# Differential attention scores on Trainium2: from 32-row fp32 products to full-height products of placed parts

## The chip, the cores and the metric

The kernel runs on one core of one Trainium2 chip. The metric is the device time of one execution in microseconds; kernels are compared by the medians of runs.

## What the kernel computes

Two transformer blocks, each two layers deep, follow one another. The first block works on 256 tokens of `x` and 256 tokens of `ctx`, 1024 features wide, in fp32. Each of its layers has a mixer with three kinds of attention heads ("a" grouped-query, "b" neighbourhood, "c" differential), and then a feed-forward network with a short convolution. The second block (FoX attention, gated linear attention and two feed-forward networks a layer) is not touched by the change.

The change concerns the four heads of kind "c". Each has two maps of 32 features, and its output is the difference of two softmaxes:

```python
def diff_attend(q, kvs, lam, scale):
    s = jnp.concatenate([jnp.einsum('bhmqd,bhmkd->bhmqk', q, k, ...) for k, _ in kvs], axis=-1) * scale
    p = jax.nn.softmax(s, axis=-1)
    w = p[:, :, 0] - lam * p[:, :, 1]
    ...
```

The 256 queries of `x` attend to the 512 keys of `x` and `ctx`; in layer 0 the 256 queries of `ctx` also attend to the 256 keys of `ctx`. In layer 1 `ctx` asks nothing.

## The kernel before

**Layout and precision.** Activations lie feature by feature: a tile has 128 features on the partitions and up to 512 tokens in its columns. A product that needs more than the reduced fp32r type gives is made of parts: `split` writes a high part (ScalarE, a copy into fp32r) and a low part (VectorE, the value less the high part). A projection of 1024 features takes 24 fp32r products (`mm1`, L269 to L271): high by high, high by low, low by high, for each of 8 blocks of 128 features. `weight` loads a block of weights on SP's queue and splits it (L261 on ScalarE, L262 on VectorE); there are four buffers of each.

**The heads of kind "c".** A tile of queries, `qc`, and one of keys, `kc`, hold two heads of two maps: 4 groups of 32 partitions. `qk` normalises and rotates them: a square (L447) and a copy (L448) on ScalarE, a product with a block matrix (L450), the root (L315 to L324), a multiplication (L452) and the rotation (L455 to L458, two of these on GpSimd). `values` copies the values to SBUF (L465), transposes them (L468) and evacuates them (`evac`, L357 on ScalarE and L359 on VectorE in turn).

**The attend loop.** `attend` runs for two heads, and in each for two blocks of 128 queries, and in layer 0 for the queries of `ctx` as well. For each of these it makes the scores of both maps (L528), the softmaxes and their difference (`weigh`: L478 to L498 on VectorE and ScalarE), calls `fill`, transposes the weights (L551, L569) and copies them out (L554, L572); at the end the weights meet the values (L579, L586). In kind "c" a score is one plain fp32 product of a 32-row slice. In the kinds "b" and "a" it is two fp32r products over 128 rows (L531, L532), of high and low parts that `stack` puts above one another with ScalarE and VectorE alone.

**What sets the order.** The first six projections run as one `gemm`. The other twelve are a generator, `project`; `fill` takes the next of them, 24 products long, wherever an attend would leave TensorE without work, and steps of the modulation (`ada_step`, L372) when there are none left. Within that the order of each engine's instructions is laid down before the run by a planner. It goes by the program's order and by the costs that it assumes, takes an instruction that is ready where an earlier one isn't, and hands out buffers. Tiles come from pools: 18 tiles of "q" (the projected tiles and stacked parts), 9 of "t" (short-lived), and in PSUM 5 banks of "mm" (projections, scores) and 3 of "at".

**The start.** `first` loads the inputs and constants, runs sixteen steps of the modulation, and then loads the first three weights of layer 0.

Of the kernel before, what the change touches and what calls it, by code (L numbers as in the profile page):

```python
# [10 lines left out]
F32R = mybir.dt.float32r  # L11
U8 = mybir.dt.uint8
AF = mybir.ActivationFunctionType
ALU = mybir.AluOpType
AX = mybir.AxisListType
P = 128
# [169 lines left out]
class Kern:  # L186
# [314 lines left out]
    def stack(self, o, n, keys):  # L501
# [13 lines left out]
                nc.scalar.activation(kl[hh][x], kl[hh][r].bitcast(F32), AF.Copy)  # L515
        return (st, kl) if keys else st

    def attend(self, l, kind, q, k, v, with_ctx, bias=None, lam=None):

        nc = self.nc  # L520
        ident = self.con("ident")
        pts = []

        def scores(sp, hh, i, qs, ks, last):

            if kind == "c":
                p0 = 64 * hh + 32 * i
                nc.tensor.matmul(sp, q[p0:p0 + 32, qs], k[p0:p0 + 32, ks], start=True, stop=last)  # L528
                return
            st, kl = k  # L530
            nc.tensor.matmul(sp, q[hh][:, qs], st[hh][:, ks], start=True, stop=False)  # L531
            nc.tensor.matmul(sp, q[hh][:, qs], kl[hh][:, ks], start=False, stop=last)  # L532

        for hh in range(2):
            maps = range(2 if kind == "c" else 1)
            px = [self.n().rearrange("p (k t) -> p k t", k=2) for _ in range(2)]
            for qi in range(2):
                sps = []
                for i in maps:
                    sp = self.mmp()  # L540
                    scores(sp, hh, i, slice(qi * P, (qi + 1) * P), slice(0, 512), bias is None)
                    if bias is not None:
                        for rr in range(2):
                            nc.tensor.matmul(sp[:, rr * P:(rr + 1) * P], self.con("rev"), bias(qi, rr, hh), start=False,
                                             stop=rr == 1)
                    sps.append(sp)
                pm = self.weigh(sps, 1, 512, lam)
                self.fill(l)
                tp = self.atp()
                for kc in range(4):  # L550
                    nc.tensor.transpose(tp[:, kc * P:(kc + 1) * P], pm[:, kc * P:(kc + 1) * P], ident)  # L551
                tv = tp.rearrange("p (k t) -> p k t", k=4)
                for i in range(2):
                    nc.vector.tensor_copy(px[i][:, :, qi * P:(qi + 1) * P], tv[:, 2 * i:2 * i + 2])  # L554
            pcx = None
            if with_ctx:
                sps = []
                for i in maps:
                    sp = self.mmp()
                    for qi in range(2):  # L560
                        scores(sp[:, qi * 256:(qi + 1) * 256], hh, i, slice(256 + qi * P, 256 + (qi + 1) * P),
                               slice(256, 512), True)
                    sps.append(sp)
                pm = self.weigh(sps, 2, 256, lam)
                self.fill(l)
                tp = self.atp()
                for kc in range(2):
                    for qi in range(2):
                        nc.tensor.transpose(tp[:, kc * 256 + qi * P:kc * 256 + (qi + 1) * P],  # L569
                                            pm[:, qi * 256 + kc * P:qi * 256 + (kc + 1) * P], ident)  # L570
                pcx = self.n()
                nc.vector.tensor_copy(pcx, tp)  # L572
            pts.append((px, pcx))
        po = self.atp()
        for kc in range(4):
            for hh, (px, pcx) in enumerate(pts):
                r0 = 64 * hh
                vv = v[:, kc * P + r0:kc * P + r0 + 64]
                nc.tensor.matmul(po[r0:r0 + 64, :256], vv, px[kc // 2][:, kc % 2], start=kc == 0,  # L579
                                 stop=kc == 3 and not with_ctx)  # L580
        if with_ctx:
            for kc in range(2):
                for hh, (px, pcx) in enumerate(pts):
                    r0 = 64 * hh
                    vv = v[:, (2 + kc) * P + r0:(2 + kc) * P + r0 + 64]
                    nc.tensor.matmul(po[r0:r0 + 64, 256:512], vv, pcx[:, kc * 256:(kc + 1) * 256], start=False, stop=kc == 1)  # L586
        return po[:, :512 if with_ctx else 256]
# [18 lines left out]
    def first_layer(self, l):  # L606
        nc, A = self.nc, self.A
# [73 lines left out]
        O = [None] * 8  # L681
        order = []
        for j in range(2):
            po = self.attend(l, "c", get("qc", j), get("kc", j), get("vc", j), wc, lam=lam)
            O[6 + j] = self.parts(self.subln(po, nq, gains["g_subln"]))
            order.append(6 + j)
        for j in range(2):
# [103 lines left out]
    def first(self, ctx):  # L791
        nc, A = self.nc, self.A
        p1 = self.p1 = self.pool(ctx, "first", 1)
        self.CON1 = p1.tile([P, NCON1], F32, name="CON1")
        self.LAM = p1.tile([P, 256], F32, name="LAM")
        self.C = p1.tile([P, KC, TC], F32, name="C")
        self.MOD = [p1.tile([P, 48, 2], F32, name=f"MOD{l}") for l in range(2)]
        self.CS = p1.tile([P, KC, 32], F32, name="CS")
        cs = self.t()[:, :KC * 32]
        nc.sync.dma_start(cs, A["ccT"].rearrange("p c i -> p (c i)"))  # L800
        nc.sync.dma_start(self.H, A["hT"])
        nc.sync.dma_start(self.C, A["cT"])
        nc.sync.dma_start(self.CON, A["con"])
        nc.sync.dma_start(self.VEC, A["vec"])
        nc.scalar.activation(self.CS.rearrange("p c i -> p (c i)"), cs, AF.Silu)
        self.table_exp()
        st = [self.stat_new(256, nc.vector), self.stat_new(256)]
        for c in range(KC):
            self.stat_add(st[0], self.H[:, c, TM:TH])
            self.stat_add(st[1], self.C[:, c, :])  # L810
        self.G1, self.G2 = {}, {}
        self.known, self.mods = -1, self.ada()
        for i in range(16):
            next(self.mods)
            if i == 7:
                with self.tc.issue_after(self.last_ada):
                    zs = [self.stat_end(s) for s in st]
                self.xn = [self.n() for _ in range(KC)]
                for c in range(KC):
                    nc.vector.tensor_tensor(self.xn[c][:, :256], self.H[:, c, TM:TH], zs[0], ALU.mult)  # L820
                    nc.vector.tensor_tensor(self.xn[c][:, 256:], self.C[:, c, :], zs[1], ALU.mult)
        self.head = [self.weight(A["w1_in"][0, j]) for j in range(3)]
        nc.sync.dma_start(self.CON1, A["con1"])
        nc.sync.dma_start(self.LAM, bass.AP(A["lamv"].tensor, 0, [[0, P], [1, 256]]))

        self.first_layer(0)
        self.first_layer(1)
# [493 lines left out]
```

## Time and profile before

| | |
|---|---|
| runs of the kernel | 2429.46 us median of 3 (2428.62 to 2435.38) |
| profiled execution | 2433.39 us; span from the first to the last instruction 2431.6 us |
| TensorE busy | 2320.8 us, 16128 matmul records |
| VectorE, ScalarE busy | 1523.2 us, 1270.2 us |
| mean granted clock of TensorE | 0.98 |
| scores of kind "c" | 82.4 to 187 us (layer 0), 762.6 to 819 us (layer 1) |

PE is TensorE, PEld its weight load, DVE VectorE, ACT ScalarE, POOL GpSimd, SP the queue that starts most transfers. L528 is line 528 of the kernel. Records of matmuls overlap, since the next starts while the last drains; what one costs in a row of them is the distance between starts.

### The profile page before, as it was taken

To read this page: it belongs to the slowest core of one execution; us is meant where nothing else is said; L and a number is where in the kernel's file an instruction comes from. 1 tells how busy PE (TensorE), PEld (TensorE's weight loads), DVE (VectorE), ACT (ScalarE), POOL (GpSimd) and SP (SyncE) were. 2 spreads that over 40 slices of the span, in tenths; PEclk is the share of its full clock that TensorE was granted. 3 is DMA by queue.
4 is the path that set the end of the run, shared out by engine and by line. 5 is a ranking of instruction groups with operands and counts; after the bars stand their busy time and mean duration, and the time that the engine had idled before them with its cause. 6 is when DMAs were issued, how large, how long until landed. Compare 5 with 4: busy or idle time off the path is not lost. (4 is left out here: it accounts for less than half of the span.)

```text
span 2431.6 us, 40872 instructions
## 1 busy us (share of the span) xinstructions
PE 2320.8 (95%) x16128; PEld 2043.5 (84%) x16128; DVE 1523.2 (63%) x2605; ACT 1270.2 (52%) x2196; POOL 401.7 (17%) x417
## 2 busy tenths in 40 slices
PE   5999999999999989999999999899999999998998
PEld 3665677778877758999999988899989999888997
DVE  4667665444547776776664876676466557666664
ACT  3658644333346775664444545554454444466553
POOL 0300021000022001211111320321121122113111
PEclk8999999999999999999999999999999999999999
DMA  7313335433233246556555533445545545334653
GB/s 269 103 37 131 113 130 173 139 121 96 93 117 120 71 156 211 194 177 191 183 168 180 167 106 105 148 157 174 174 148 178 169 147 195 104 114 149 196 180 118
DMA packets 100993, 358.57 MB, mean 147 GB/s; under 512 B 11488, under 2 KB 12864, under 8 KB 100544
## 3 DMA queue, kind: packets, MB, share of 16 engines
q1 hardware_dynamic: 98640, 349.82, 44.4%
q0 software_dynamic: 1792, 5.53, 0.9%
q8 instruction: 127, 2.08, 0.4%
q10 hardware_dynamic: 368, 0.59, 0.1%
q14 instruction: 66, 0.54, 0.1%
HBM read 354.83 MB, written 1.07 MB: 146 GB/s over the span
## 5 line engine op out<-in xcount | busy, mean ns | idle before, releaser
L269 PE MATMUL mm_t<-n_t,hi_t 128*128 128x272 f32 (+2 forms) x3600 | 1112.4, 310 | 25.4 <-ACT n_t L839 18.7
L270 PE MATMUL mm_t<-n_t,hi_t 128*128 128x272 f32 (+2 forms) x3600 | 1109.5, 308 | 6.0 <-DVE n_t L840 5.0
L271 PE MATMUL mm_t<-n_t,lo_t 128*128 128x272 f32 (+2 forms) x3600 | 1106.0, 308 | 1.1 <-DVE lo_t L262 1.1
L262 DVE TENSOR_TENSOR lo_t<-raw_t,hi_t 128x1024 fp32r<-128x1024 f32 (+1 forms) x574 | 713.2, 1246 | 391.2 <-ACT hi_t L261 387.1
L261 ACT ACTIVATE hi_t<-raw_t 128x1024 fp32r<-128x1024 f32 (+1 forms) x574 | 595.5, 1039 | 680.6 <-PE mm_t L270 509.4
L269 PEld LDWEIGHTS mm_t<-n_t,hi_t 128*128 128x128 f32 x3600 | 686.0, 191 | 77.7 <-ACT n_t L839 20.9
L270 PEld LDWEIGHTS mm_t<-n_t,hi_t 128*128 128x128 f32 x3600 | 688.5, 191 | 38.1 <-DVE n_t L840 8.4
L271 PEld LDWEIGHTS mm_t<-n_t,lo_t 128*128 128x128 f32 x3600 | 687.9, 191 | 33.0 <-issue 5.8
L269 PE MATMUL mm_t<-q_t,hi_t 128*128 128x272 f32 (+2 forms) x896 | 274.6, 307 | 0.7 <-ACT q_t L306 0.7
L270 PE MATMUL mm_t<-q_t,hi_t 128*128 128x272 f32 (+2 forms) x896 | 274.4, 306 | 0.0
L271 PE MATMUL mm_t<-q_t,lo_t 128*128 128x272 f32 (+2 forms) x896 | 274.3, 306 | 0.0
L343 POOL TENSOR_TENSOR t_t<-t_t 128x272 f32<-128x272 f32 (+1 forms) x108 | 122.9, 1143 | 540.2 <-ACT t_t L339 515.2
L269 PEld LDWEIGHTS mm_t<-q_t,hi_t 128*128 128x128 f32 x896 | 168.4, 188 | 8.8 <-ACT q_t L306 1.1
L270 PEld LDWEIGHTS mm_t<-q_t,hi_t 128*128 128x128 f32 x896 | 168.9, 188 | 7.6 <-DVE q_t L307 0.2
L271 PEld LDWEIGHTS mm_t<-q_t,lo_t 128*128 128x128 f32 x896 | 168.9, 189 | 7.5
L888 POOL TENSOR_TENSOR t_t<-t_t 128x272 f32<-128x272 f32 (+1 forms) x88 | 75.6, 860 | 443.3 <-DVE t_t L882 386.9
L738 POOL TENSOR_TENSOR t_t<-t_t 128x512 f32<-128x512 f32 (+1 forms) x44 | 56.7, 1288 | 442.2 <-ACT t_t L737 442.2
L882 DVE TENSOR_TENSOR t_t<-mm_t,t_t 128x272 f32<-128x272 f32 (+1 forms) x176 | 75.6, 436 | 64.2 <-PE mm_t L271 62.4
L372 PE MATMUL at_t<-raw_t,CS 128*32 128x256 f32 x768 | 70.6, 431 | 35.7 <-DMA raw_t<-in_w_ada_dram 35.4
L307 DVE TENSOR_TENSOR q_t<-t_t,q_t 128x272 fp32r<-128x272 f32 (+2 forms) x112 | 55.8, 498 | 73.4 <-ACT q_t L306 73.4
L306 ACT ACTIVATE q_t<-t_t 128x272 fp32r<-128x272 f32 (+2 forms) x112 | 52.3, 467 | 90.4 <-POOL t_t L738 47.8
L480 ACT ACTIVATE t_t<-mm_t,s_t 128x512 f32<-128x512 f32 (+1 forms) x120 | 72.7, 607 | 26.5 <-DVE s_t L478 25.7
(253 smaller groups left out, 2146.9 us busy)
## 6 DMA issues: line engine op xcount, KB each, us to landing
raw_t<-in_w_up_dram SPq DMA_DIRECT2D x264, 512.0 KB, 3.3
raw_t<-in_w_in_dram SPq DMA_DIRECT2D x118, 512.0 KB, 3.4
raw_t<-in_w_ada_dram SPq DMA_DIRECT2D x96, 512.0 KB, 4.4
raw_t<-in_w_dn_dram SPq DMA_DIRECT2D x96, 448.0 KB, 3.3
raw_t<-in_w_dn_dram SPq DMA_DIRECT2D x48, 512.0 KB, 3.6
raw_t<-in_w_out_dram SPq DMA_DIRECT2D x32, 512.0 KB, 3.4
raw_t<-in_w_fg_dram SPq DMA_DIRECT2D x16, 512.0 KB, 3.3
q_t<-cum POOLq DMA_DIRECT2D x8, 272.0 KB, 7.4
```

Source lines behind the costliest of these rows:

```text
L261: nc.scalar.activation(hi[:, :k], raw[:, :k], AF.Copy)
L262: nc.vector.tensor_tensor(lo[:, :k], raw[:, :k], hi[:, :k].bitcast(F32), ALU.subtract)
L269: self.nc.tensor.matmul(ps, wh, xh, start=start, stop=False)
L270: self.nc.tensor.matmul(ps, wh, xl, start=False, stop=False)
L271: self.last_mm = self.nc.tensor.matmul(ps, wl, xh, start=False, stop=stop).ins
L307: self.nc.vector.tensor_tensor(lo, src, hi.bitcast(F32), ALU.subtract)
L343: st.eng.tensor_tensor(st.acc, st.acc, sq, ALU.add)
L372: self.last_ada = nc.tensor.matmul(ps[32 * g:32 * g + 32], self.CS[:, k, :], wv[:, g], start=k == 0, stop=k == KC - 1).ins
L480: nc.scalar.activation(pm[:, i * nk:(i + 1) * nk], sp[:, i * nk:(i + 1) * nk], AF.Exp, bias=m[:, i:i + 1], accum_out=sm[:, i:i + 1])
L738: nc.gpsimd.tensor_tensor(u, u, g, ALU.mult)
L882: nc.vector.tensor_tensor(u, ps, z[0], ALU.mult)
L888: nc.gpsimd.tensor_tensor(u, u, g, ALU.mult)
```

## The change

The slice products of kind "c" are replaced. A new function `stack4` splits a whole tile of queries or keys into high and low parts, and makes for each of the four groups of 32 partitions one tile of 128 rows. For queries these rows hold high, high, low, low; for keys high, low, low, high. One product over all 128 rows is then the sum of all four products of parts. The rows are put in place by TensorE: each tile is two accumulated fp32r products, of the high and of the low part, with 128 columns of `SEL`. `SEL` holds, for each group, columns of the identity in blocks of 32 and zeros between, so that different cuts of it place a part differently. Four banks of a call are evacuated by ScalarE and VectorE in turn. `SEL` is filled once, by sixteen ScalarE copies placed after the modulation steps of `first`. A score becomes one fp32r product of two such tiles.

```diff
+    def stack4(self, o, n, keys):
+        nc = self.nc
+        hi, lo = self.t(F32R)[:, :n], self.t(F32R)[:, :n]
+        self.split(o[:, :n], hi, lo)
+        res = []
+        for g in range(4):
+            ps = self.mmp()[:, :n]
+            for i, x in enumerate((hi, lo)):
+                b = 32 * (2 * i + (1 if keys else 0))
+                w = self.SEL[:, g, b:b + P]
+                nc.tensor.matmul(ps, w, x, start=i == 0, stop=i == 1)
+            st = self.q(F32R)[:, :n]
+            self.evac(st, ps)
+            res.append(st)
+        return res
+
     def attend(self, l, kind, q, k, v, with_ctx, bias=None, lam=None):
...
             if kind == "c":
-                p0 = 64 * hh + 32 * i
-                nc.tensor.matmul(sp, q[p0:p0 + 32, qs], k[p0:p0 + 32, ks], start=True, stop=last)
+                nc.tensor.matmul(sp, q[2 * hh + i][:, qs], k[2 * hh + i][:, ks], start=True, stop=last)
                 return
...
-            po = self.attend(l, "c", get("qc", j), get("kc", j), get("vc", j), wc, lam=lam)
+            po = self.attend(l, "c", self.stack4(get("qc", j), nq, False), self.stack4(get("kc", j), 512, True), get("vc", j), wc,
+                             lam=lam)
...
+        self.SEL = p1.tile([P, 4, 224], F32R, name="SEL")
+        sel = self.SEL.rearrange("p g (b r) -> p g b r", r=32)
+        for g in range(4):
+            rows = self.con("ident")[:, 32 * g:32 * g + 32].unsqueeze(1).to_broadcast([P, 2, 32])
+            for b, x in ((0, 1.0), (2, 0.0), (4, 1.0)):
+                nc.scalar.activation(sel[:, g, b:b + 2], rows, AF.Copy, scale=x)
+            nc.scalar.activation(sel[:, g, 6], rows[:, 0], AF.Copy, scale=0.0)
         self.head = [self.weight(A["w1_in"][0, j]) for j in range(3)]
```

## Rows read from the trace of the kernel before

**Rows 1.** The page, busy time of each engine: us, share, instructions.

```profile
PE 2320.8 (95%) x16128; PEld 2043.5 (84%) x16128; DVE 1523.2 (63%) x2605; ACT 1270.2 (52%) x2196; POOL 401.7 (17%) x417
```

**Rows 2.** Busy time by stretch, then TensorE's clock, DMA share, GB/s.

```profile
82.00:188.00 106.00, 100.59 (x438) 68.78 (x437) 71.07 (x146) 67.76 (x137) 19.96 (x22) 0.98 0.19 55
188.00:280.00 92.00, 81.65 (x590) 50.95 (x588) 74.10 (x171) 80.05 (x187) 2.84 (x4) 0.98 0.47 161
762.00:830.00 68.00, 63.06 (x324) 44.26 (x322) 50.08 (x106) 45.91 (x92) 17.46 (x18) 1.00 0.30 93
```

**Rows 3.** Busy time by stretch of line L528 alone (TensorE, weight load).

```profile
82.00:188.00 106.00, 16.92 (x64) 6.40 (x64) 0.98 0.19 55
762.00:830.00 68.00, 9.02 (x32) 2.39 (x32) 1.00 0.30 93
```

**Rows 4.** Timeline of TensorE at 100 us: start, length, instruction, idle before it.

```profile
100.23 0.39 PE L271 MATMUL mm_t<-n_t,lo_t 128*128 128x512 f32 x1
100.55 1.14 PE L528 MATMUL mm_t<-q_t 32*128 32x256 f32 x8
102.03 0.66 PE L468 MATMUL at_t<-CON,t_t 128*128 128x128 f32 x4 [0.34 <-ACT t_t L465]
```

**Rows 5.** Timeline of TensorE at 165 us.

```profile
164.68 0.39 PE L271 MATMUL mm_t<-n_t,lo_t 128*128 128x512 f32 x1
165.00 1.12 PE L528 MATMUL mm_t<-q_t 32*128 32x512 f32 x2
166.05 1.13 PE L450 MATMUL at_t<-t_t,CON 128*128 128x512 f32 x2
```

**Rows 6.** Timeline of TensorE, first and last product of two projections.

```profile
102.88 0.48 PE L269 MATMUL mm_t<-n_t,hi_t 128*128 128x512 f32 x1
...
108.19 0.39 PE L271 MATMUL mm_t<-n_t,lo_t 128*128 128x512 f32 x1
...
839.20 0.28 PE L270 MATMUL mm_t<-n_t,hi_t 128*128 128x256 f32 x1
...
841.83 0.28 PE L271 MATMUL mm_t<-n_t,lo_t 128*128 128x256 f32 x1
```

**Rows 7.** Timeline of ScalarE, and of TensorE's transpose, at 82 us.

```profile
82.28 1.06 ACT L261 ACTIVATE hi_t<-raw_t 128x1024 fp32r<-128x1024 f32 x1 [1.64 <-PE mm_t L270]
83.25 0.58 ACT L465 ACTIVATE t_t<-mm_t 128x512 f32<-128x512 f32 x1
...
83.88 0.66 PE L468 MATMUL at_t<-CON,t_t 128*128 128x128 f32 x4 [0.35 <-ACT t_t L465]
```

**Rows 8.** TensorE's waits, 82 to 190 and 762 to 830 us: total, times, longest.

```profile
PE at_t L450 <- ACT t_t L447: 3.0, 5, 1.6
PE at_t L468 <- ACT t_t L465: 2.4, 4, 1.4
...
PE at_t L450 <- ACT t_t L447: 2.4, 4, 1.5
PE at_t L468 <- ACT t_t L465: 2.1, 3, 1.2
```

**Rows 9.** Evacuations of 128 by 512 by tile: min/median/max in ns.

```profile
L357 ACT ACTIVATE q_t<-at_t x3: 597/599/601, 71.2 to 157.8; 128x512 f32<-128x512 f32 x3
...
L359 DVE COPY q_t<-at_t x2: 679/681/683, 86.2 to 128.1; 128x512 f32<-128x512 f32 x2
```

**Rows 10.** Timeline of TensorE where the first "b" heads begin.

```profile
194.55 1.12 PE L450 MATMUL at_t<-t_t,CON 128*128 128x512 f32 x2 [1.62 <-ACT t_t L447]
...
199.46 0.85 PE L531 MATMUL mm_t<-q_t 128*128 128x512 f32 x3 [0.60 <-ACT q_t L512]
```

**Rows 11.** Timeline of ScalarE before the first weight splits.

```profile
28.77 0.42 ACT L317 ACTIVATE t_t<-t_t 128x256 f32<-128x256 f32 x1
40.64 0.38 ACT L377 ACTIVATE t_t<-at_t 128x256 f32<-128x256 f32 x1 [11.45 <-PE at_t L372]
```

**Rows 12.** Busy time by stretch, with the granted clock, at 158 us.

```profile
158.00:160.00 2.00, 2.00 (x8) 1.71 (x7) 2.00 (x5) 1.56 (x6) 0.00 (x0) 0.50 0.04 4
```

## The prediction

> **What bounds the kernel now.** I read the page's busy table first [rows 1]: TensorE is busy for 95% of the span, so a change counts where it alters what TensorE does or waits for. Then I took the busy time of each engine in the stretches where the scores of kind "c" are made, 82 to 188 us (layer 0) and 762 to 830 us (layer 1), and of the "b" and "a" heads behind the first [rows 2]. The reader should see that TensorE is busy for 100.6 of 106 us and 63.1 of 68 us there, at full clock or nearly so, while VectorE and ScalarE have about a third free each; the idle TensorE time of both stretches together is only 10 us. What fills TensorE is not the scores: between them stand the input projections that `fill` brings in, 24 products each. The score line itself, L528, covers 16.9 us of TensorE in layer 0 and 9.0 us in layer 1 [rows 3]. The change touches only these some 175 us and a few instructions at the start; the other nine tenths of the program stay as they are. The profiled execution took 2433.39 us, 3.9 us (0.16%) over the median of 2429.46; I sum changes against it and put the result on the median.
>
> **What is removed.** 32 products of 512 columns and 16 of 256, each in two records (96 records for 48 products). Two products on different 32-row groups run side by side: the stretch at 100.55 holds eight records, four products, and takes 1.14 us [rows 4]; the one at 165.00 holds one product in two records and takes 1.12 us [rows 5]. So a pair costs what one costs. In the program's order they form 23 stretches: in layer 0 six pairs, three fours, four single 512-wide products and two stretches of two 256-wide ones on one row group; in layer 1 eight pairs.
>
> The skill speaks against the change here. In the Trainium skill, "TensorE: Matmul & The Clock Gate", Part 3, a product over 32 rows takes as long as one over 128, and what small contractions gain is that tiles run at once. The trace agrees (1.12 us for one, 1.13 for two). Counted product by product, the 14 pairs and three fours would take twice their time and leave another 17 x 1.05 = 18 us to win; by the rule, and by the rows, those are not there.
>
> After the change each product is one full-height fp32r matmul. The nearest rows are the projections: 24 products of 512 columns start from 102.88 to 108.19 us, 0.23 us apart, and 23 of 256 columns from 839.20 to 841.83, 0.12 us apart [rows 6]. So 32 x 0.23 + 16 x 0.12 = 9.3 us replace L528.
>
> How much of the difference reaches the end depends on what stands behind each stretch. I walked the TensorE timeline through all 23:
> - Eight stretches (the six of layer 0 that hold one row group alone and the pairs of layer 1 at 762.6 and 785.4) are followed by TensorE's own work without a wait. At 165.00 the next instruction starts 1.05 us after the stretch began, and the stretch began 0.32 us after the product before it, which itself needs 0.23 [rows 5]. The new product takes 0.23, so 1.05 + 0.09 - 0.23 = 0.91 us is freed. Six of these give 5.4 us, and the two pairs about 0.7 each: **6.8 us firm**.
> - Fifteen stretches end in a wait for ScalarE. At 100.55 the next start is 1.48 us later, of which 0.34 is a wait for L465 [rows 4]. What sets that is not the score: the weight split L261 of a later tile waits for the end of the projection ahead, then takes 1.06 us, and L465 or L447 queue behind it in ScalarE's order, so the transpose at 83.88 starts just after L465's end at 83.83 [rows 7]. Such waits, with one at 828.9 us that is behind other work, sum to 5.4 us in layer 0 and 4.5 in layer 1 [rows 8]. A shorter score only lengthens such a wait, unless the new order puts other TensorE work into it. Bounds: 0, and 15 x (1.48 + 0.09 - 0.46) = 16.7 us. I take 5, nearer the lower end, since ScalarE is the late party in the rows, and because some filling is likely: the order is made by a planner that puts ready work into holes.
>
> **What is added.** (1) Placing: eight calls of `stack4`, each with 8 fp32r products by columns of the identity. Six calls have 512 columns and two (layer 1's queries) 256: 6 x 8 x 0.23 + 2 x 8 x 0.12 = **12.9 us** on TensorE [rows 6]. Since TensorE is nearly full, I count all of it. (2) Each call also brings one split (ScalarE copy, VectorE subtraction) and four evacuations, turn by turn. A 512-wide evacuation takes 0.60 us on ScalarE and 0.68 on VectorE [rows 9]; with the split that is at most 1.8 us of ScalarE and 2.1 of VectorE a call, 14 and 16 us over eight calls. Their cover is the third of the stretch in which each is idle [rows 2]; without it they would cost those 14 to 16 us. (3) The wait that this brings: scores of the first head need two key parts, hence split, product and evacuation for queries and keys, and the five banks of the matmul pool can't hold the eight placed parts together with a projection and score pairs. The trace has no such step. Below: nothing, if the planner places the parts while the head before is still at work. Above: about 3 us for each of the four pairs of calls, with nothing else for TensorE to do: 1.3 us of split ahead of the first product (0.60 and 0.68) and two evacuations in turn on one engine, 1.3 us, behind the last. The nearest rows are the first "b" heads, which also build stacked operands first: TensorE waits 1.62 and 0.60 us there [rows 10]. I take 0.5 us a pair, **2 us**, because the later pair of a layer can be placed early; bounds 0 and 12. (4) Sixteen small ScalarE copies that fill `SEL`. ScalarE is idle for 11.45 us before 40.64 us, waiting for TensorE, and a 256-wide activation there takes 0.38 us [rows 11]; 16 of them, at most 6 us, fit. I cost them at nothing; if they stood behind 40.64 us they would delay the first weight split, and cost up to 6 us. (5) The old q and k tiles die earlier, but eight stacked ones live through an attend; the pool of 18 still holds the six fills. Nothing.
>
> **Sum.** -6.8 - 5 + 12.9 + 2 = +3.1 us. On the median: 2429.5 + 3 = **2432.5 us**.
>
> **The rivals.**
> *Faster: TensorE is simply the bound.* All freed time counts, nothing waits: -6.8 - 16.7 + 12.9 = -10.6 us, 2419 us. For it: TensorE is 95% busy in the stretches [rows 2], and the planner fills holes it foresees. Against: 15 of 23 stretches end on ScalarE, and ScalarE gets more to do.
> *Slower: the placed parts wait for their evacuations.* Place: the start of each attend, four times. Price: up to 3 us each with no wait refilled, -6.8 + 12.9 + 12 = +18 us, 2447.5 us. It passes the limit of no change when the waits come to more than 0.3 us a pair with nothing refilled, or about 1.5 us a pair with the 5 us refilled. For it: the waits of [rows 10]; temps and banks held by the split parts. Against: the projections stand ready as other work.
> *The change doesn't do what it says:* that scores get no shorter, because the new product would be ruled by its weight load. The rows of equal shape contradict it: L269 to L271 load weights for each product and still start 0.23 us apart [rows 6]. Then nothing would be freed, and 12.9 + 2 us added: 2444 us.
>
> **How the numbers follow.** 0.3% of 2429 us is 7.3 us, about what a measurement of this kernel can tell from no change. The forecast, a change within that band, has 0.5; the faster rival beyond the band 0.2; the slower rival 0.28; no shorter scores 0.02. Hence faster 0.2, same 0.5, slower 0.3. Half of the faster and most of the slower cases lie close to the band, so the range runs from 2419 (all freed time counts) to 2445, short of the worst ends. A moved idle stretch can also bring or drop a spell of half clock, as at 158 to 160 us [rows 12]: some 2 us either way, within the range.
>
> **What the profile after would show.** L528 with 48 records of 128 rows, 0.23 us apart, no second records, and about 9 us where it had 26; 64 new products on the placing line, some 13 us; ScalarE and VectorE up by 12 to 16 us in the two stretches; the stretch from 82 us ending within some 4 us of 188, and that from 762 shifted by as much. The waits of L450 and L468 for ScalarE would grow if the scores were covered, and shrink if the holes are refilled. The copies for `SEL` stand before 40 us. Wrong would be: TensorE idle for more than 2 us ahead of the first score of an attend (the slower rival), or the two stretches shorter by over 4 us each (the faster one), or the placing products riding wholly in waits that the trace has now.

## The result, and the profile after

The changed kernel takes 2456.15 us (median of 4 runs, 2455.17 to 2457.43), beside 2430.44 us for the kernel before in the same series: a ratio of 1.010, 95% interval 1.0086 to 1.0114. It is 25.7 us, or 1%, slower. The forecast of 2432.5 us is 23.7 us off, and the range ended 11 us below the result.

The helper `stack4` shifts the lines behind it by 18: the scores of kind "c" are L546 after (L528 before), the placing products L531, the value products L597 (L579 before). The page's busy line of the kernel after stands beside [rows 1]:

```profile
PE 2326.9 (95%) x16144; PEld 2058.8 (84%) x16144; DVE 1538.5 (63%) x2629; ACT 1284.9 (52%) x2236; POOL 400.7 (16%) x417
```

TensorE's busy time rises by 6 us only, VectorE's by 15.3, ScalarE's by 14.7. The span rises by 23.4 us (2455.0 against 2431.6), so most of the added time is not time in which TensorE is busy. The scores did get shorter. Busy time of L546 alone, and then of the placing line L531 alone, in the stretches that hold them (answering to [rows 3]):

```profile
80.00:205.00 125.00, 7.81 (x32) 5.47 (x32) 0.96 0.16 47
770.00:850.00 80.00, 5.28 (x16) 2.88 (x16) 0.93 0.29 88
...
80.00:205.00 125.00, 10.74 (x32) 7.74 (x32) 0.96 0.16 47
770.00:850.00 80.00, 10.49 (x32) 7.36 (x32) 0.93 0.29 88
```

48 score records take 13.1 us where 96 took 25.9; the 64 placing products take 21.2. That is more than 13, and the stretches' mean clock, 0.96 and 0.93, hints at why.

To see where the time goes I cut both traces at the same events: from the first square of the head norm (L447) of a layer to the first value product of its last attend (in layer 1 the cut lies 0.74 us ahead of that square, in every profile alike). Busy time by stretch, with TensorE first and its mean granted clock third from the end, of the kernel before and then of the kernel after:

```profile
62.11:290.52 228.41, 212.65 (x1176) 142.24 (x1174) 165.59 (x353) 169.58 (x365) 27.57 (x30) 0.99 0.31 102
745.01:914.32 169.31, 157.88 (x970) 113.29 (x968) 124.21 (x285) 124.01 (x252) 26.98 (x30) 0.98 0.36 116
```

```profile
61.03:301.95 240.92, 212.40 (x1178) 148.76 (x1176) 174.76 (x365) 176.35 (x377) 28.17 (x30) 0.96 0.30 97
752.46:936.87 184.41, 165.45 (x986) 122.72 (x984) 130.56 (x297) 129.70 (x264) 25.20 (x30) 0.94 0.33 107
```

Layer 0's heads are 12.5 us longer, layer 1's 15.1, together 27.6 us. (Outside these stretches the profiled execution after is 4.2 us shorter: 1.1 us ahead of the first, 4.0 between the two, -0.9 behind. The stretch between them took 450.0 to 454.7 us in the fourteen profiles of this study and 454.5 in the one of before, so the 4 us lie within what profiles differ by there.) TensorE's idle time is length less busy time: 15.8 and 11.4 us before, 28.5 and 19.0 after. The busy time holds some at half clock, and the trace's record of the granted clock says how much: 6.8 and 6.1 us before, 13.3 and 18.6 after. Half of that is counted as what half clock costs, an estimate (the placing products below start 0.427 us apart at half clock and 0.234 at full). So the 27.6 us are made up as

| kernel | length | = idle | + half-clock cost | + TensorE's work at full clock |
|---|---|---|---|---|
| after, layer 0 | +12.5 | +12.8 | +3.2 | -3.5 |
| after, layer 1 | +15.1 | +7.5 | +6.2 | +1.3 |
| after, sum | +27.6 | +20.3 | +9.5 | -2.2 |

(us against before; work is length less idle less half of the half-clock busy time.) The change left TensorE 2 us less to do and 30 us of idle time and half clock. The timeline of TensorE shows where the idle time is. In layer 0 of the kernel before, the first scores came right behind the last projection, which started at 82.08, and the scores of the second attend came ahead of the first attend's value products (L579):

```profile
82.40 1.13 PE L528 MATMUL mm_t<-q_t 32*128 32x512 f32 x4
...
133.37 1.13 PE L528 MATMUL mm_t<-q_t 32*128 32x512 f32 x4
...
136.34 1.95 PE L579 MATMUL at_t<-n_t,q_t 128*64 128x256 f32 x16
```

The same two places in the kernel after:

```profile
80.99 0.39 PE L271 MATMUL mm_t<-n_t,lo_t 128*128 128x512 f32 x1
82.78 0.66 PE L468 MATMUL at_t<-CON,t_t 128*128 128x128 f32 x4 [1.41 <-ACT t_t L465]
83.28 1.12 PE L450 MATMUL at_t<-t_t,CON 128*128 128x512 f32 x2
87.02 0.50 PE L531 MATMUL mm_t<-t_t,SEL 128*128 128x512 f32 x1 [2.62 <-ACT t_t L306]
89.72 6.25 PE L531 MATMUL mm_t<-t_t,SEL 128*128 128x512 f32 x15 [2.21 <-DVE t_t L307]
95.81 0.62 PE L546 MATMUL mm_t<-q_t 128*128 128x512 f32 x2
...
138.27 0.39 PE L271 MATMUL mm_t<-n_t,lo_t 128*128 128x512 f32 x1
140.07 1.13 PE L450 MATMUL at_t<-t_t,CON 128*128 128x512 f32 x2 [1.41 <-ACT t_t L447]
...
141.56 1.95 PE L597 MATMUL at_t<-n_t,q_t 128*64 128x256 f32 x16
...
145.07 1.12 PE L613 MATMUL at_t<-t_t,CON 128*128 128x512 f32 x2 [0.70 <-ACT t_t L610]
148.15 3.99 PE L531 MATMUL mm_t<-t_t,SEL 128*128 128x512 f32 x16 [1.96 <-ACT t_t L306]
151.98 0.39 PE L546 MATMUL mm_t<-q_t 128*128 128x512 f32 x1
```

14.8 us pass from the last projection to the first score, of which TensorE waits 6.2: for the values' copy (L465), for the high part (L306) and for the low part (L307). Nothing stands between L450 and the placing in TensorE's order. The second start, from 138.27 on, shows a second loss: the scores of the second attend come 10.4 us behind the first attend's value products, where before they came 3 us ahead of them (133.37 and 136.34). The four starts take 14.8, 13.7, 12.1 and 12.8 us, with 6.2, 4.1, 5.2 and 3.4 us of waiting, 18.9 in all. Of these, 11.8 us are waits for the split, which the kernel before doesn't have. The other 7.1 are for steps that it has too: L447, L465, L572 and L610, the first two of which it waits for at other places ([rows 8]).

Why the parts are late, from ScalarE's and then VectorE's timeline:

```profile
83.11 0.69 ACT L448 ACTIVATE q_t<-mm_t,gq_c 128x512 f32<-128x512 f32 x1
84.43 0.69 ACT L315 ACTIVATE t_t<-at_t,eps 128x512 f32<-128x512 f32 x1 [0.64 <-PE at_t L450]
85.15 0.63 ACT L316 ACTIVATE t_t<-t_t 128x512 f32<-128x512 f32 x1
85.81 0.63 ACT L317 ACTIVATE t_t<-t_t 128x512 f32<-128x512 f32 x1
86.35 1.13 ACT L306 ACTIVATE t_t<-q_t 128x512 fp32r<-128x512 f32 x2
```

```profile
87.20 0.69 DVE L324 SCALAR_TENSOR_TENSOR t_t<-t_t 128x512 f32<-128x512 f32 x1
87.92 0.69 DVE L452 TENSOR_TENSOR q_t<-q_t,t_t 128x512 f32<-128x512 f32 x1
...
88.66 0.43 DVE L455 STREAM_SHUFFLE t_t<-q_t 128x256 f32<-128x256 f32 x1
88.99 0.68 DVE L307 TENSOR_TENSOR t_t<-q_t,t_t 128x512 fp32r<-128x512 f32 x1
```

The split is queued behind the norm of the last head tile: L306 behind the roots L315 to L317, L307 behind L320 to L455. That norm waits in turn for TensorE's own L450. So TensorE waits for a chain that it has itself just started, and no other work stands in its order. At the end of that wait the clock is down, as the stretches of the same seconds show (TensorE first, its granted clock third from the end):

```profile
88.00:90.00 2.00, 0.28 (x1) 0.28 (x2) 1.63 (x4) 0.00 (x0) 0.76 (x1) 0.60 0.00 0
90.00:92.00 2.00, 2.00 (x5) 1.54 (x6) 1.02 (x3) 0.60 (x1) 2.00 (x4) 0.50 0.00 0
92.00:94.00 2.00, 2.00 (x6) 1.59 (x5) 1.30 (x3) 0.63 (x2) 0.48 (x1) 0.50 0.50 131
```

TensorE is busy throughout from 90 to 94 us, at 0.50 of its clock, that is 1.2 GHz. Most of the 15 placing products there start 0.427 us apart; those at 148.15, at full clock, 0.234. The Trainium skill ("TensorE: Matmul & The Clock Gate", Part 1) gives 427 ns between starts of 512 columns at 1.2 GHz; the trace agrees. Half clock begins likewise at 774.5 and 815.4 us, in the starts of layer 1, and at 201.0 us, in a wait of 5.1 us that answers to the 1.62 us of [rows 10]; e2 below, which places nothing, has it too. The kernel after, and then e2:

```profile
203.54 2.08 PE L450 MATMUL at_t<-t_t,CON 128*128 128x512 f32 x2 [5.09 <-ACT t_t L447]
...
185.53 2.08 PE L450 MATMUL at_t<-t_t,CON 128*128 128x512 f32 x2 [5.11 <-ACT t_t L447]
```

### The profile page after: what moved, and what is told of

Read it like the earlier page. It is cut to its first block, busy times and chain, and to the rows that moved or that the text cites. A ratio compares the mean times of both kernels' runs of the same rounds, so it can differ in the third digit from the quotient of the medians.

```text
span 2455.0 us, 40973 instructions
## 1 busy us (share of the span) xinstructions
PE 2326.9 (95%) x16144; PEld 2058.8 (84%) x16144; DVE 1538.5 (63%) x2629; ACT 1284.9 (52%) x2236; POOL 400.7 (16%) x417
## 5 line engine op out<-in xcount | busy, mean ns | idle before, releaser
L307 DVE TENSOR_TENSOR q_t<-t_t,q_t 128x272 fp32r<-128x272 f32 (+2 forms) x112 | 55.8, 498 | 72.4 <-ACT q_t L306 72.4
L372 PE MATMUL at_t<-raw_t,CS 128*32 128x256 f32 x768 | 69.3, 429 | 32.3 <-DMA raw_t<-in_w_ada_dram 31.8
L306 ACT ACTIVATE q_t<-t_t 128x272 fp32r<-128x272 f32 (+2 forms) x112 | 52.3, 467 | 89.3 <-POOL t_t L757 48.5
```

The lines of the kernel that those rows point to most:

```text
L307: self.nc.vector.tensor_tensor(lo, src, hi.bitcast(F32), ALU.subtract)
L372: self.last_ada = nc.tensor.matmul(ps[32 * g:32 * g + 32], self.CS[:, k, :], wv[:, g], start=k == 0, stop=k == KC - 1).ins
```

## The experiments

All runs are compared with the kernel before on the same chip (medians 2432.1 to 2432.9 us). The changed kernel was timed in the first series alone, beside 2430.44 us; where a run's median is set against its 2456.15 us, differences of two or three us decide nothing. I began with two theories: the chain (split, placing and evacuation one behind the other at each start, with TensorE idle and then at half clock), and its rival, the evacuations and the PSUM banks. Each expectation words its own theories; a letter holds for that run. The last column of the table says how the two stages together differ from before in the profile, cut as above.

| run | time, ratio (95%) | stages: length = idle + half clock + work |
|---|---|---|
| kernel after | 2456.15, 1.010 (1.0086-1.0114) | +27.6 = 20.3 + 9.5 - 2.2 |
| e1 projection drawn ahead | 2464.09, 1.0136 (1.0115-1.0157) | +36.4 = 19.9 + 13.1 + 3.4 |
| e2 no placing | 2429.66, 0.9991 (0.9981-1.0000) | -0.5 = 10.1 + 5.7 - 16.3 |
| e3 first split early | 2453.44, 1.0090 (1.0072-1.0108) | +23.5 = 17.5 + 7.9 - 1.9 |
| e4 both placed early | 2468.45, 1.0160 (1.0136-1.0184) | +43.1 = 33.0 + 10.2 - 0.1 |
| e5 first pair only | 2440.55, 1.0041 (1.0023-1.0058) | +9.8 = 5.5 + 3.6 + 0.7 |
| e6 idle time filled | 2452.70, 1.0086 (1.0064-1.0107) | +24.6 = 12.3 + 3.0 + 9.4 |
| e7 long scores | 2471.03, 1.0155 (1.0130-1.0180) | +39.6 = 15.4 + 3.1 + 21.1 |
| e8 hidden | 2448.52, 1.0076 (1.0050-1.0101) | +23.7 = 13.6 + 7.5 + 2.6 |
| e9 second pair only | 2443.74, 1.0042 (1.0027-1.0057) | +17.9 = 12.2 + 8.0 - 2.3 |
| e10 second pair early | 2455.15, 1.0086 (1.0071-1.0101) | +26.7 = 19.3 + 6.8 + 0.6 |
| e11 high parts alone | 2452.57, 1.0073 (1.0054-1.0091) | +21.0 = 19.8 + 8.6 - 7.4 |
| e12 one group placed | 2460.89, 1.0108 (1.0091-1.0125) | +29.6 = 25.2 + 16.1 - 11.7 |

**e1: a projection as filler.** One more projection is drawn ahead of each pair of calls, to stand in the wait.

```diff
+            next(self.project)
             po = self.attend(l, "c", self.stack4(get("qc", j), nq, False), ...
```

> One projection is drawn ahead of each of the four pairs of stack4 calls, so that TensorE has 5.5 us of work while the split is made. Theory A (TensorE stands idle at each start of a head pair because the split comes late out of ScalarE and VectorE, and then runs at half clock): the 6.2 us and some 5 us of idle ahead of the placing products shrink to under 2 us, the placing products run 0.23 us apart, and the time falls from 2456 to 2434 to 2442 us. Rival B (the placed parts wait for banks and evacuations): products 0.4 us apart or more still, 2452 us or more. Rival C (the loss is made later, by the added ScalarE and VectorE work and the moved order of the b and a heads): the starts improve, the end does not, 2450 us or more.

Slower than the changed kernel: the theory that a filler in the wait wins the time back missed. Waiting at the four starts did fall, from 18.9 to 11.8 us (3.4, 1.6, 4.4, 2.4). But there are twelve projections in all, and each one used here is missing later: TensorE's idle time over the stages stays at +19.9 us, and its half clock grows. In layer 0 TensorE now waits 5.8 us for the weights of the modulation steps that fill in for projections (L372; 0.4 us in the changed kernel).

**e2: shorter scores without placing.** A call is one ScalarE copy into the high part, used whole for all four groups; the low parts, the placing and its evacuations are left out, and groups are mixed.

```diff
...
+    def half(self, o, n):
+        hi = self.q(F32R)[:, :n]
+        self.nc.scalar.activation(hi, o[:, :n], AF.Copy)
+        return [hi] * 4
...
```

> Leaves out the low parts and the placing: a score is one fp32r product of the high parts over all 128 rows, which mixes the groups, and a call of stack4 is one ScalarE copy. Theory A: what is left is the gain of the shorter scores, 7 to 18 us, 2412 to 2424 us. Rival C: the loss between the last c scores and the b heads (about 7 us in layer 0) is there without placing too, since it comes from the shorter scores, and the time is 2425 to 2437 us.

This is the gain side, as nearly as a run shows it, and it is hardly there: 2.4 us off a median of 2432.1, while TensorE's work falls by 16.3 us. The rest comes back as idle time (+10.1, of which 4.4 are waits for this run's own copies at the two first starts, 2.33 and 2.11) and half clock (+5.7). With 16.3 us of work gone and no placing at all, the kernel gains about 0.1%. It is not the gain of the scores alone: beside those copies, e2 keeps the later second start (in layer 0 the second attend's scores come 2.7 us behind the first attend's value products). So a placing that cost nothing would have gained little in this order of the work; the shorter scores without the copies and in the old order were not run.

**e3: the first split earlier.** The first pair's split stands right behind its two projections.

```diff
...
+            if i == 2:
+                early["q"], early["k"] = self.cut2(T["qc"][0], nq), self.cut2(T["kc"][0], 512)
...
```

> The split of the first pair of each layer is made right behind its own projections; placing products and evacuations stay where they are, and so does the second pair. Theory A: the idle ahead of the first placing product falls by about 5 us in each layer and the half clock behind it goes, 2438 to 2446 us. Rival B: no change at the first scores, 2453 us or more.

The first score of layer 0 comes at 90.8 us and not 95.8, but the gain at the end is 2.7 us (the intervals overlap). The wait for the split is gone, and others take its place, as TensorE's timeline at the same start shows:

```profile
83.77 0.66 PE L468 MATMUL at_t<-CON,t_t 128*128 128x128 f32 x4 [1.08 <-ACT t_t L465]
...
84.81 1.95 PE L535 MATMUL mm_t<-t_t,SEL 128*128 128x512 f32 x6
89.76 1.19 PE L535 MATMUL mm_t<-t_t,SEL 128*128 128x512 f32 x4 [3.00 <-DVE q_t L359]
```

Now the placing line (L535 here) waits 3.0 us for an evacuation to free a bank. That evacuation on VectorE is behind the same norm as the split was. The rival's wait exists, but only once the first one is out of its way.

**e4: both pairs placed early.** The first pair is placed behind its projections, the second at the first attend's third fill, with 19 tiles in the pool.

```diff
...
+            if i in (2, 8):
+                j = i // 8
+                S.append((self.stack4(T["qc"][j], nq, False), self.stack4(T["kc"][j], 512, True)))
...
```

> All of stack4 moves: the first pair is placed right behind its projections, the second at the third fill of the first pair's attend; the pool of heads has 19 tiles for 18. Theory A: both waits at the starts go, 2425 to 2440 us. If tiles or banks are what placing waits for, it waits in the middle of the attend instead, and the time stays above 2448 us.

The slowest but one. The placing now stands in front of head projections that are still to come, and TensorE waits 3.58 us for L465 and 7.62 for L306 there, with the mean clock at 0.54 from 65 to 80 us.

**e5 and e9: one pair at a time.** In e5 the first two heads of a layer keep placed parts and the second two go back to 32-row products; in e9 it is the other way round.

```diff
...
-            po = self.attend(l, "c", self.stack4(get("qc", j), nq, False), self.stack4(get("kc", j), 512, True), get("vc", j), wc,
-                             lam=lam)
+            pair = (self.stack4(...), self.stack4(...)) if j == 0 else (get("qc", j), get("kc", j))
+            po = self.attend(l, "c", *pair, get("vc", j), wc, lam=lam)
```

> The first two heads of a layer keep placed parts; the other two go back to 32-row fp32 products, so two of the four starts have no split, no placing and no evacuation, and the second attend's first scores stand ahead of the first attend's value products again. Theory A (each start pays a serial chain of split, placing and evacuation, with TensorE idle, and often half clock behind it): the price adds up start by start, and about half of the 25 us goes: 2438 to 2446 us. Theory B (the price comes from the first start of a layer alone, and the rest only follows from it): nothing to speak of goes, 2450 us or more.

> The other half of the run with the first pair alone: the first two heads of a layer go back to 32-row fp32 products, the second two keep placed parts. That run left 8 us over the kernel before, of some 25. If the price adds up start by start, this one is 15 to 19 us over the kernel before (2447 to 2451 us), and the second start is the dearer, since its parts stand behind the first attend's value products. If the second start costs only because the first has used up the projections that would have filled its wait, this one is 5 to 10 us over (2438 to 2442).

e5 came out as the chain wants it: 7.8 us over before. With the second pair back on 32 rows, its scores stand ahead of the first attend's value products again, as TensorE's timeline of e5 shows (L550 the scores, L601 the value products):

```profile
139.66 1.13 PE L550 MATMUL mm_t<-q_t 32*128 32x512 f32 x4
...
142.63 1.95 PE L601 MATMUL at_t<-n_t,q_t 128*64 128x256 f32 x16
```

e9's median is 10.9 us over before, less than the 15 to 19 expected and just above the other theory's 5 to 10. The stages of the two profiles do add up: +9.8 and +17.9, 27.7 together, where both pairs cost 27.6. The medians, 7.8 and 10.9, fall 7 short of 25.7; between single profiles and medians of a few runs I can't decide that, so the sharing by start is roughly 1 to 1.4 or 1 to 1.8. That each start has a price of its own, and that it is not one of the first start alone, both measures show; that the two prices add up to the whole, only the stages do.

**e6: the idle time filled.** Twelve products of constants that nothing reads stand ahead of each placing.

```diff
...
+            idle = self.mmp().rearrange("p (a b) -> p a b", b=256)[:, :, :224]
+            with self.tc.issue_after(self.last_ms):
+                for i in range(12):
+                    nc.tensor.matmul(idle, self.SEL[:, 0, :P], self.SEL[:, 0:2, :], start=True, stop=True)
```

> Twelve products of 448 columns that nothing reads, made of constants, are added ahead of each placing, where TensorE idles for 3 to 6 us in the changed kernel; the result is unchanged. If half clock behind the idle time is a part of the price (15 placing products took 6.25 us at the start of layer 0 where a row at full clock takes 3.5), the placing products stand 0.23 us apart at all four starts, and the time falls by 3 to 7 us: 2449 to 2453. If the chain of ScalarE and VectorE alone sets the time, the clock there makes no difference: 2455 to 2458. If TensorE's time counts there in full, the added 10 us make it slower: 2460 or more.

About 10 us of work were added, and the time fell by 3.5 us, though the intervals overlap. Against the changed kernel the stages have 11.6 us more work, 8.0 less idle time and 6.5 less half clock. At the second starts the placing products stand 0.23 us apart as expected (the 256-wide ones of layer 1 0.12); at the first starts a wait for the low part stays (1.51 and 0.92 us in layer 0), and the clock falls behind it all the same:

```profile
86.46 1.21 PE L531 MATMUL mm_t<-t_t,SEL 128*128 128x512 f32 x4 [0.19 <-ACT t_t L306]
89.17 1.43 PE L531 MATMUL mm_t<-t_t,SEL 128*128 128x512 f32 x5 [1.51 <-DVE t_t L307]
91.52 3.35 PE L531 MATMUL mm_t<-t_t,SEL 128*128 128x512 f32 x7 [0.92 <-DVE t_t L307]
```

So work of TensorE's own in those waits is free, up to the length of the wait. Half clock is a part of the price by the profile's account, and the time lies in the range that was expected of that; the medians alone, whose intervals overlap, don't show it.

**e7: longer scores.** Each score is a plain fp32 product over the 128 placed rows.

```diff
-                nc.tensor.matmul(sp, q[2 * hh + i][:, qs], k[2 * hh + i][:, ks], start=True, stop=last)
+                nc.tensor.matmul(sp, q[2 * hh + i][:, qs].bitcast(F32), k[2 * hh + i][:, ks].bitcast(F32), start=True, stop=last)
```

> Placing as in the changed kernel, but each score is a plain fp32 product over the 128 placed rows: longer on TensorE by some 0.9 us for each of the 512-wide ones and 0.45 us for the 256-wide ones, 32 x 0.9 + 16 x 0.45 = 36 us of TensorE. If a score's length counts in full, as the firm part of the prediction has it, the time rises by 30 us or more: 2486. If the scores are covered by the softmax on ScalarE and VectorE, as the run without placing suggests (18 us fewer gave 2 us), it rises by 5 to 12 us: 2461 to 2468.

Between the two theories. The expectation had the longer score too long: its two records start 0.43 us apart, so a 512-wide score takes 0.86 us and not the 1.1 of a 32-row one, and L546 is busy for 38.7 us in place of 13.1, 25.6 more and not 36. The stages have 23.3 us more work than the changed kernel's and are 12.0 us longer, since 4.9 us of idle time and 6.4 of half clock go; the medians differ by 14.9. In either direction a part of what TensorE gains or loses in its scores is given back by the waits around them: half here, nearly all in e2.

**e8 and e10: hiding the chain.** In e8 the first pair is split early as in e3, one projection is drawn ahead of its placing, and the second pair is split and placed at the first attend's third fill. e10 has the last of these alone, and one fill later than its expectation says: its placing hangs on the same projection (`i == 9`), and as none is drawn ahead, that is the fourth fill, in layer 1 the last of the attend.

```diff
...
+            if i == 9:
+                S.append((self.stack4(T["qc"][1], nq, False), self.stack4(T["kc"][1], 512, True)))
...
```

> An attempt to hide the chain: the first pair is split right behind its projections and one projection is drawn ahead of its placing; the second pair is split and placed inside the first attend, at its third fill, with 19 tiles in the pool. Theory A (waits at the starts): with the waits hidden, what stays is the 12.9 us of placing less the little that shorter scores give: 2436 to 2446 us. Theory C (the fill is the scarce thing, so whatever is drawn early is missed later): no better than the changed kernel, 2450 us or more.

> The first pair is split and placed as in the changed kernel; the second pair is split and placed inside the first attend, at its third fill, with 19 tiles in the pool. If the second start is dear for its place in the order alone (scores of the second attend behind the value products of the first), its price falls to that of its products, 6.4 us, and the time to 2440 to 2445 us. If the parts delay the first attend by as much, as seen when both pairs were moved, 2448 us or more.

e8 is the best version that keeps placed parts for all four heads, 7.6 us faster than the changed kernel, and still 15.7 us over before: it reached neither theory's range. e10 is no better than the changed kernel (1.0 us, intervals overlapping). In both, the time from the first attend's value products in layer 0 to the second's shrinks (64.8 us in the changed kernel, 58.2 in e8, 55.9 in e10, 59.7 before), so the second start of layer 0 is repaired. But the first attend's value products come 8.4 and 8.6 us later. The parts wait wherever they stand; at its new place in e10 the placing looks like this:

```profile
125.33 1.12 PE L450 MATMUL at_t<-t_t,CON 128*128 128x512 f32 x2 [1.41 <-ACT t_t L447]
126.29 0.60 PE L569 MATMUL at_t<-CON,t_t 128*128 128x128 f32 x4
128.41 3.34 PE L531 MATMUL mm_t<-t_t,SEL 128*128 128x512 f32 x12 [1.52 <-ACT t_t L306]
131.82 0.50 PE L546 MATMUL mm_t<-q_t 128*128 128x512 f32 x1
133.02 1.19 PE L531 MATMUL mm_t<-t_t,SEL 128*128 128x512 f32 x4 [0.70 <-DVE t_t L307]
```

**e11 and e12: less of the chain.** e11 leaves the low parts out: one copy, four placing products and four evacuations a call. e12 keeps the split and leaves three of the four groups out: two placing products and one evacuation a call, one tile for all four operands. The edit of e12:

```diff
-        for g in range(4):
+        for g in range(1):
...
-        return res
+        return res * 4
```

> The low parts are left out: a call makes one ScalarE copy, four placing products in place of eight and four evacuations; the order of the starts stays. It takes 6.4 us of TensorE and the VectorE subtraction away (the wait for it was 2.2 us at the start of layer 0). If split, products and evacuations stand one behind the other and each counts, the time falls by 12 to 16 us, to 2440 to 2444. If evacuations and order set it, by less than 6 us: 2450 or more.

> Three of the four groups are left out: a call makes the whole split, two placing products in place of eight and one evacuation in place of four, and all four score operands are that one tile; the order of the starts stays. It takes 9.7 us of TensorE and three quarters of the evacuations away. If the placing products and their evacuations are the price, the time falls by 10 to 14 us, to 2442 to 2446. If the split and its waits are, by less than 6 us: 2450 or more. What stays over the run without placing (2429.7) is then the price of the splits and of the order.

e11 gave 3.6 us, and its stages are 6.6 us shorter than the changed kernel's, 5.2 of them TensorE's work: what was taken out counts there, and hardly any waiting goes. With the low parts gone, an evacuation on VectorE (L359) is the late party, as TensorE's timeline of e11 shows at the first start of layer 0 (L529 the placing):

```profile
92.49 0.73 PE L529 MATMUL mm_t<-t_t,SEL 128*128 128x512 f32 x2 [3.06 <-DVE q_t L359]
```

It stands behind the same norm: VectorE runs L320 to L455 of the last head tile until 89.83 and its L458 from 91.41, and starts that evacuation at 91.75. So whichever step of the placing VectorE has first, the split or an evacuation, waits there for the norm.

e12 gave nothing (4.7 us slower than the changed kernel, intervals overlapping), with six of eight products and three of four evacuations gone from each call. The four starts together are 3.6 us shorter (49.8 against 53.4), so the number of products and evacuations sets little of their length. In e12 the stages have 9.5 us less work than the changed kernel's, and 4.9 us more idle time and 6.6 more half clock. TensorE's timeline at the first start of layer 0, and the stretches behind it:

```profile
87.24 0.50 PE L531 MATMUL mm_t<-t_t,SEL 128*128 128x512 f32 x1 [2.62 <-ACT t_t L306]
89.96 1.22 PE L531 MATMUL mm_t<-t_t,SEL 128*128 128x512 f32 x2 [2.22 <-DVE t_t L307]
92.29 0.79 PE L531 MATMUL mm_t<-t_t,SEL 128*128 128x512 f32 x1 [1.11 <-DVE t_t L307]
93.96 1.19 PE L546 MATMUL mm_t<-q_t 128*128 128x512 f32 x2 [0.88 <-DVE q_t L359]
```

```profile
92.00:95.00 3.00, 1.83 (x4) 1.16 (x5) 1.17 (x3) 0.00 (x0) 0.71 (x1) 0.50 0.36 87
95.00:98.00 3.00, 3.00 (x9) 2.32 (x8) 1.95 (x6) 2.06 (x5) 2.59 (x3) 0.50 0.02 7
```

With twelve of sixteen placing products gone, the first score comes 1.85 us earlier (93.96 against 95.81); the splits take as long as they did. Then the scores and projections run at 1.2 GHz until 99.2 us by the trace's record of the clock, where the changed kernel is back at full clock at 95.2. In the changed kernel the products that e12 leaves out keep TensorE busy from 90 to 96 us; in e12 it is busy for 1.83 us from 92 to 95.

## Why the prediction was wrong

**The step that failed is the term "added (3)", the wait that placing brings**, taken as 0.5 us a pair of calls, 2 us, with a bound of 3 us a pair. Measured: 6.2, 4.1, 5.2 and 3.4 us of waiting at the four starts, 18.9 us, of which 11.8 are for the split itself. Set against e2, which has the shorter scores and places nothing, the stages of the changed kernel are 28.1 us longer: 14.1 of TensorE's work, 10.2 of idle time and 3.8 of half clock. So beside its own products placing cost 14.0 us, where the sum had 2. The term's bound was built from the split's own durations and two evacuations. It left out what the split is queued behind: the norm of the last head tile, which the prediction had read as other work on an engine with a third of its time free (for VectorE in layer 1 it is a quarter: 50.1 of 68 us are busy in [rows 2]). The reason given for a low value, that the later pair can be placed early, fell as well: in the laid-down order it stands behind the first attend's value products, and e10 shows that moving it up pays next to nothing.

**A second step failed by nearly as much: "what is removed"**, summed at 11.8 us, gave 2.4 in e2. Of the 22.6 us between the forecast change of 3.1 and the measured 25.7, that is 9.4; the wait that placing brings, half clock included, is 12.0, and its products are the other 1.2. The border between the two is not sharp: e2's own copies wait 4.4 us at the two first starts, and up to that much could belong to placing.

**Half clock was taken at 2 us either way; it costs 9.5 us.** [Rows 12] showed that a spell of it occurs, and the prediction did not add it to the stalls that it forecast. Of the 9.5 us, e2 has 5.7 without any placing, so 3.8 are left to placing itself. In e6 useless work took the place of idle time and half clock at no loss; in e12, with less work, both grew.

**What is removed.** TensorE's work fell by 16.3 us in e2, between the 6.8 us held firm and the 23.5 of the upper bound; the 11.8 us summed are too few as work and far too many as time. As time it was worth 2.4 us, less than the 6.8 called firm, though e2's copies (4.4 us) keep that run from refuting the 6.8 alone. What does speak against it is the wait at 203.54: a stretch followed by TensorE's own work frees that work, but a little later TensorE waits the longer for ScalarE. The six firm stretches of layer 0 stand right ahead of it, and it grew from 1.62 to 5.1 us, by 3.5 of their 5.4; e2, without placing, has the same wait (5.11 us at 185.53). So the next wait behind such a stretch decides, not what stands right behind it.

**What was right.** Placing is 14.1 us of TensorE's work (the stages after against those of e2; 12.9 predicted). Scores start 0.23 us apart in 48 records, so the rival "doesn't do what it says" is out. VectorE and ScalarE are up by 15.3 and 14.7 us (16 and 14 predicted). The copies for `SEL` cost nothing: they run from 13.8 to 16.1 us, and the first weight split starts at 39.3 us, against 40.9 before. The tile pool held up.

**The rivals.** The slower rival had place and sign right: TensorE is idle for more than 2 us ahead of the first score of every attend. Its mechanism was not the one at work: at the four starts of the changed kernel no wait is for an evacuation; 11.8 us are for the split (L306, L307), 5.0 for the copies L447 and L465, the other 2.1 for L610 and L572. In e3 and e11, where a part of the split is out of the way, an evacuation is the late party (3.0 and 3.1 us). Its 12 us at most would have held those 11.8, but its sum of 2447.5 us is 8.7 short of the result, as it too counts the 6.8 us as gained and no half clock. The faster rival, TensorE as the bound, is contradicted by e2.

Two things stay open. How the price divides between first and second starts is known only within the two measures of e5 and e9. And some half clock of layer 1 (849 to 890 us in the changed kernel) lies in attends that the change doesn't touch; I take it for a consequence of the shifted waits, as e2 has some there too (820 to 861 us), but no run separates it.

## What to carry to other kernels

When operands are to be prepared just ahead of the work that needs them, cost the whole chain from the last result to the first use, with everything queued ahead of it on each engine, and ask what the busy engine has in its order meanwhile; durations of the new instructions alone gave 2 us for 14 us of idle time and half clock. A TensorE that is 95% busy can still be paced by others at its joints: test with the new work left out (e2) before building it, since 16 us less to do gave 2.4. And a stall is paid a second time where half clock follows it.

## What the runs showed that I had not expected

Useless products were free: some 10 us of them in the waits made the kernel no slower (2452.7 against 2456.15 us). Taking 9.5 us of real TensorE work away made it no faster (2460.89), because the same wait stayed and TensorE ran longer at 1.2 GHz behind it: 45.0 us of busy time at half clock over the two stages, against 31.8 in the changed kernel and 12.8 before. In e11, though, 5.2 us less work made the stages 6.6 us shorter, so the outcome of less work at a start depends on the wait that is left.
